# One block of a streaming encoder on one core: kept tiles' products tied to the gate matmuls on TensorE's queue, another first pair of groups for the dense stage, and GpSimd's share of the gate operands

## The chip, the cores and the metric

The kernel runs on one core of a Trainium2 chip. The metric is device microseconds for one execution; the kernel before was timed in three runs. PE is TensorE, DVE VectorE, ACT ScalarE, POOL GpSimd, SP the engine whose queue issues most plain DMAs.

## The reference, cut to what matters

The block computes a token mixer (an mLSTM beside a forgetting attention) and then a product-key expert layer (PEER) over 1024 tokens. The change touches only the PEER layer:

```python
# x: (1024, 1024); u_emb, v_emb: (16384, 1024)
scores = einsum('thpc,hpnc->thpn', (xb @ w_query), keys)     # 8 heads, 2 halves, 128 keys
val, idx = top_k(scores, 16)
top_s, pos = top_k(val[:, :, 0, :, None] + val[:, :, 1, None, :], 16)
ids  = idx0 * 128 + idx1 at pos                              # 8*16 = 128 experts per token
gate = softmax(top_s)
act  = gelu(einsum('ted,td->te', u_emb[ids], xb))
out  = einsum('te,ted->td', gate * act, v_emb[ids])
```

An expert's number is i * 128 + j. All is float32.

## The kernel before

The 1024 tokens are four segments of 256 (`SEGS`, two blocks of 128 tokens each). Segments 0 and 3 take the expert layer sparsely: each block gathers its 128 rows of u and 128 rows of v per token with indirect DMAs that POOL issues (`gather_rows`, L328, L364, L395), and DVE or PE uses them (L337, L386, L410). Segments 1 and 2 (512 tokens together, `DENSE`) take it densely: for each of 128 *tiles* of 128 experts, PE makes the 128 x 512 products of u with the tokens, ACT applies gelu, DVE multiplies by a dense table of gates, and PE multiplies the result with the tile's rows of v.

A tile's products cost 24 matmuls (`feat_proj`, L292): every fp32 operand is split into a high part on ACT (`wh`, L281) and a low part (`wl`, on DVE at L286, or for every third on POOL at L284), and three products are made for each of eight slices. Of the 128 tiles 60 are *kept* (`SPILL`): their products are made early (`spill`, L1025), copied out of PSUM by ACT (L1027) and stored to DRAM (`wsd`). 36 of the 60 are made while segment 3 is mixed, 24 in the stage after it. The other 68 (`rest`) are made in the dense stage itself by `dense_u` (L1204).

The stage around the change is the `merge` at L1214, from about 1600 us to 2038 us. It interleaves three generators in program order: the top-k of segment 3 (8 steps), 24 kept tiles, and `all_gates` (16 steps). `merge` takes next the generator with the smallest (steps done + 0.5) / cost; the costs of kept tiles and gates are 24 and 16.

`gates` builds the dense table for segments 1 and 2. For four tokens at a time (a *quad*; 128 quads, eight to a step) it makes four one-hot operands B in one DVE instruction (L1171) and four operands A: the last by two ACT instructions (L1176, L1177), the others by DVE or POOL (L1180); how many POOL makes is `GPOOL`, one of four for segment 1 and none for segment 2. Four matmuls (L1182, eight records in the trace) form the quad in one PSUM bank, and ACT copies it into `G` (L1184). A and B have two buffers. After eight quads `G` goes to DRAM (`gd`, L1186, 2 MB).

The dense stage takes the tiles in 32 groups of four. The list `order` begins with two kept groups (`FIRST`) and then takes rest and kept in proportion. `dense_u` is called five tiles ahead (`AHEAD`), `acc` (the residual of the 512 tokens) is loaded (L1246), and then, group by group, `weights` loads that group's gates (`Gt`, L1252), multiplies and splits them (L1256 to L1260), further `dense_u` follow, and `dense_v` splits the rows of v and runs 96 matmuls (L1278), which DVE adds to `acc` (L1283). `beat` hands out 1.08 of the 512 gathers of segment 3 per beat, and each waits for the PE instruction last recorded in `seen["pe"]`.

The order on each engine's queue is not the program order: a planner lists instructions by priority (program order, unless `high_priority`) over a modelled timeline, and the queues then run in that fixed order, each waiting on semaphores. `tc.issue_after(x)` makes the planner put the instructions of the block that run on x's engine behind x; it adds no wait of its own. The gate matmuls stand under `high_priority`.

Of the kernel before, what the change touches and what calls it, by code (L numbers as in the profile page):

```python
# [19 lines left out]
P = 128  # L20
# [29 lines left out]
SHARE = 3  # L50
GRP = 4
AHEAD = 5
FIRST = 2
XB = 4
XU = 1
TOP0 = (0, 1, 0, 1)
SW = 1
GP0 = 5

GPOOL = (1, 0)  # L60
T3W = 1.2
GW = 1
T00 = 0
# [30 lines left out]
def _block_kernel(ctx, tc, nc, I, out, dbg):  # L94
# [44 lines left out]
    dve, act, pe, pool_e, sync = nc.vector, nc.scalar, nc.tensor, nc.gpsimd, nc.sync  # L139
# [102 lines left out]
    h2d = dp.tile([SEQ, D], F32, tag="h2d", name="h2d")  # L242
    xnd = dp.tile([SEQ, D], F32, tag="xnd", name="xnd")

    Xh = big.tile([P, KT, 2 * NX], F32R, tag="xh", name="xh")
    Xl = big.tile([P, KT, 2 * NX], F32R, tag="xl", name="xl")
# [6 lines left out]
    def rawt(name):  # L253
        return wp.tile([P, L], F32, tag="raw", name=name, bufs=RAW)
# [20 lines left out]
    def halves(src, share=0, tiles=1):  # L275

        raw = rawt("raw")[:, 0:1024]
        sync.dma_start(raw.rearrange("p (i c) -> p i c", i=tiles) if tiles > 1 else raw, src)
        h = wpart("wh")
        l = wpart("wl")  # L280
        seen["act"] = act.copy(h, raw)  # L281
        turn[0] += 2
        if share and turn[0] % (2 * share) == 0:
            pool_e.tensor_sub(l, raw, h.bitcast(F32))  # L284
        else:
            seen["dve"] = dve.tensor_sub(l, raw, h.bitcast(F32))  # L286
        return [(h[:, i * 512:(i + 1) * 512], l[:, i * 512:(i + 1) * 512]) for i in range(2)]
# [6 lines left out]
    def feat_proj(wsrc, xh, xl, c, o=None, share=0):  # L294

        if xl is not None:
            u = halves(wsrc, share)
        else:
            raw = rawt("raw")[:, 0:KT * P]
            sync.dma_start(raw, wsrc)  # L300
        if o is None:
            o = acc_bank("fp")[:, 0:c.stop - c.start]
        if xl is None:
            for k in range(KT):
                pe.matmul(o, raw[:, k * P:(k + 1) * P], xh[:, k, c], start=(k == 0), stop=(k == KT - 1))  # L305
            return o
        for k in range(KT):
            h, l = u[k // 4]
            kc = slice(k % 4 * P, (k % 4 + 1) * P)
            mm3(o, c, h[:, kc], l[:, kc], xh[:, k, :], xl[:, k, :], k == 0, k == KT - 1)  # L310
        return o
# [707 lines left out]
    DX = 2 * NX  # L1019
    wsd = dp.tile([P, P, DX], F32, tag="wsd", name="wsd")  # L1020

    def spill(lo, hi):

        for i in range(lo, hi):
            a = feat_proj(I["ut"][i], Xh, Xl, slice(0, DX), share=SHARE)  # L1025
            t = ring("spill")[:, 0:DX]
            act.copy(t, a)  # L1027
            sync.dma_start(wsd[i], t)
            yield
# [101 lines left out]
    nb, xb0, nx = 2 * NB, sum(SEGS[:DENSE[0]]), DX  # L1131
# [4 lines left out]
    def gates(S, gb):  # L1136

        for b in range(NB):
            hi = gb.tile([P, P], I32, tag="gi", name="gi_hi")
            lo = gb.tile([P, P], I32, tag="gi", name="gi_lo")  # L1140
            dve.tensor_scalar(hi, S.idx[:, b, :], 7, None, op0=OP.logical_shift_right)
            dve.tensor_scalar(lo, S.idx[:, b, :], 127, None, op0=OP.bitwise_and)
            T = []
            for x, nm in ((hi, "iT"), (lo, "jT"), (None, "gT")):
                if x is None:
                    f = S.gate[:, b, :]
                else:
                    f = gb.tile([P, P], F32, tag="gf", name="gf", bufs=1)
                    dve.tensor_copy(f, x)
                tb = bank("gtr")  # L1150
                with tc.high_priority():
                    pe.transpose(tb[:, 0:P], f, ident)
                t_ = gb.tile([P, P], F32, tag=nm, name=nm, bufs=1)
                act.copy(t_, tb[:, 0:P])
                T.append(t_)
            iT, jT, gT = T
            niT = gb.tile([P, P], F32, tag="niT", name="niT", bufs=1)
            act.mul(niT, iT, -1.0)
            ngT = gb.tile([P, P], F32, tag="ngT", name="ngT", bufs=1)
            act.mul(ngT, gT, -1.0)  # L1160
            for tg in range(P // TG):
                G = gb.tile([P, P, TG], F32, tag="G", name="G")
                for q in range(TG // 4):
                    bk = dps.tile([P, 512], F32, tag="db", name="gout")
                    t0 = tg * TG + q * 4
                    ts4 = slice(t0, t0 + 4)
                    A = gb.tile([P, 4, P], F32, tag="A", name="A")
                    B = gb.tile([P, 4, P], F32, tag="B", name="B")
                    bc = [P, 4, P]
                    io = iota.unsqueeze(1).broadcast_to(bc)  # L1170
                    dve.tensor_tensor(B, io, jT[:, t0:t0 + 4].unsqueeze(2).broadcast_to(bc), op=OP.is_equal)  # L1171
                    for u in range(4):
                        t1 = slice(t0 + u, t0 + u + 1)
                        if u == 3:

                            act.activation(A[:, u, :], iota, AF.Abs, bias=niT[:, t1])  # L1176
                            act.activation(A[:, u, :], A[:, u, :], AF.Relu, bias=gT[:, t1], scale=ngT[:, t1])  # L1177
                        else:
                            e = pool_e if u < GPOOL[S.sg - DENSE[0]] else dve
                            e.tensor_scalar(A[:, u, :], iota, iT[:, t1], gT[:, t1], op0=OP.is_equal, op1=OP.mult)  # L1180
                        with tc.high_priority():
                            pe.matmul(bk[:, u * P:(u + 1) * P], B[:, u, :], A[:, u, :], start=True, stop=True)  # L1182
                    with nullcontext():
                      act.copy(G[:, :, q * 4:q * 4 + 4].rearrange("p i t -> p t i"),  # L1184
                             bk.rearrange("p (t i) -> p t i", t=4))
                sync.dma_start(gd[:, :, (NB * (S.sg - DENSE[0]) + b) * (P // TG) + tg, :].rearrange("g j c -> j g c"),  # L1186
                               G.rearrange("p (g i) t -> p g (i t)", i=GRP))
                yield


    kept, rest = list(range(sum(SPILL) // GRP)), list(range(sum(SPILL) // GRP, P // GRP))
    order = kept[:FIRST]
    kept = kept[FIRST:]
    while kept or rest:
        order.append((kept if len(kept) * (P // GRP) >= len(rest) * (P // GRP) and kept else rest).pop(0))

    def dense_u(i):
        i = order[i // GRP] * GRP + i % GRP
        w = up.tile([P, 512], F32, tag="w", name="w")
        if i < sum(SPILL):  # L1200
            sync.dma_start(w, wsd[i])
            act.activation(w, w, AF.Gelu)
        else:
            a = feat_proj(I["ut"][i], Xh, Xl, slice(0, nx), acc_bank("du"))  # L1204
            act.activation(w, a, AF.Gelu)  # L1205
        return w
# [24 lines left out]
    def beat(n=1):  # L1231

        count[0] += n * RATE
        k, count[0] = int(count[0]), count[0] % 1
        pace.step(seen["pe"], k)

    ws = []
    for i in range(AHEAD):
        ws.append(dense_u(i))
        beat(2)  # L1240

    ds_ = pool("dense", 2, reuse_waits="tile")
    xs0 = xb0 * P
    acc = ds_.tile([P, nb, D], F32, tag="acc", name="acc", bufs=1)
    for b in range(nb):
        sync.dma_start(acc[:, b, :], h2d[xs0 + b * P:xs0 + (b + 1) * P, :])  # L1246

    def weights(g):

        res = []  # L1250
        Gt = ds_.tile([P, nx // TG, GRP, TG], F32, tag="Gt", name="Gt", bufs=2)
        sync.dma_start(Gt, gd[order[g]].rearrange("j b (i t) -> j b i t", i=GRP))  # L1252
        for ii in range(GRP):
            w = ws[g * GRP + ii]
            w3 = w.rearrange("p (b t) -> p b t", t=TG)
            dve.tensor_mul(w3, w3, Gt[:, :, ii, :])  # L1256
            Wh = ds_.tile([P, 512], F32R, tag="Wh", name="Wh", bufs=2 * GRP)
            Wl = ds_.tile([P, 512], F32R, tag="Wl", name="Wl", bufs=2 * GRP)
            act.copy(Wh, w)  # L1259
            dve.tensor_sub(Wl, w, Wh.bitcast(F32))  # L1260
            res.append((Wh, Wl))
        return res

    def dense_v(g, W):
        for d in range(2):
            cv = slice(d * 512, (d + 1) * 512)
            bks = [bank("vo") if b < 2 else dps.tile([P, 512], F32, tag="db", name="vo") for b in range(nb)]
            for ii in range(GRP):
                if ii % 2 == 0:

                    e0 = (order[g] * GRP + ii) * P
                    v2 = halves(I["peer_v"][e0:e0 + 2 * P, cv].rearrange("(i p) c -> p i c", p=P), tiles=2)
                Wh, Wl = W[ii]
                vh, vl = v2[ii % 2]
# [10 lines left out]
    NG = P // GRP  # L1285
    for g in range(NG):
        W = weights(g)
        for i in range(len(ws), min(P, (g + 1) * GRP + AHEAD)):
            ws.append(dense_u(i))
            beat(2)  # L1290
        dense_v(g, W)
    pace.end()
# [50 lines left out]
```

## Time and profile before

| | |
|---|---|
| timed runs | 3248.06, 3258.47, 3261.81 us; median 3258.47 |
| profiled execution | 3247.17 us, span 3245.2 us |
| PE busy | 2943.9 us, 91% |
| DVE busy | 2345.9 us, 72% |
| POOL busy | 1407.1 us, 43% |
| ACT busy | 1047.9 us, 32% |
| DMA | 937.42 MB, 289 GB/s over the span |

The shares are means over stages that differ. PE's row by slices (each 81 us long) shows where it isn't full; the windows and waits of such a stretch then show what it waits for. A matmul's duration in a row overlaps with its neighbours', so the pace of PE is read from the distance of starts.

### The profile page before, as it was taken

The page shows a single profiled execution, that of the slowest core. Times are in us where ns is not written, and L with a number is a line of the kernel's source. Part 1 is how long each engine was busy: PE and PEld are TensorE (multiplying, and loading weights), DVE is VectorE, ACT ScalarE, POOL GpSimd, SP SyncE. Part 2 cuts the span into 40 slices and gives each one's busy share as a digit, 9 for nine tenths or more (in the row PEclk, how much of TensorE's full clock was granted, in tenths as well). Part 3 has the DMA queues.
Part 4 walks back from the last instruction along what each step waited for, and adds up shares of the span by engine and source line. Part 5 has one row for each costly group of instructions (what it writes and reads, how often), then busy time and mean ns, then how long its engine had stood idle before and what let it go on. Part 6 is the DMA issues. An engine that isn't in the chain of part 4 may idle for free. (4 is left out here: it accounts for less than half of the span.)

```text
span 3245.2 us, 40750 instructions
## 1 busy us (share of the span) xinstructions
PE 2943.9 (91%) x13711; PEld 2174.8 (67%) x13711; DVE 2345.9 (72%) x5633; ACT 1047.9 (32%) x1946; POOL 1407.1 (43%) x1221
## 2 busy tenths in 40 slices
PE   8999898667977889999899996898999999999998
PEld 4566566544654667776467885677777776777776
DVE  3342599997546897556467997788988877787787
ACT  1323323222222222222156666222332222232221
POOL 1000053554556654346465202345555555545454
PEclk9988998788979789999999997999999999999999
DMA  4534578998999978889997568889999998999888
GB/s 130 148 101 125 181 264 263 341 339 299 347 303 376 316 272 254 254 262 346 344 327 234 178 190 277 309 297 347 364 354 358 354 349 335 350 361 351 324 338 291
DMA packets 379317, 937.42 MB, mean 289 GB/s; under 512 B 57652, under 2 KB 143892, under 8 KB 375012
## 3 DMA queue, kind: packets, MB, share of 16 engines
q0 software_dynamic: 161216, 552.56, 47.9%
q1 hardware_dynamic: 217892, 382.25, 34.5%
q8 instruction: 108, 1.77, 0.2%
q14 instruction: 101, 0.83, 0.1%
HBM read 864.06 MB, written 70.62 MB: 288 GB/s over the span
## 5 line engine op out<-in xcount | busy, mean ns | idle before, releaser
L328 POOL DMA_INDIRECT gu<-in_peer_u,idx x512 | 626.1, 1223 | 622.0 <-PE vo L1278 123.5
L337 DVE SCALAR_TENSOR_TENSOR gu<-gu,xng 128x1024 f32<-128x1024 f32 x512 | 621.0, 1229 | 82.3 <-DMA gu<-in_peer_u,idx 81.2
L364 POOL DMA_INDIRECT gv<-in_peer_v,idT x384 | 426.0, 1109 | 410.4 <-PE po L386 193.4
L281 ACT CAST wh<-raw 128x1024 fp32r<-128x1024 f32 x288 | 301.3, 1048 | 674.2 <-PE vo L1278 329.4
L286 DVE TENSOR_TENSOR wl<-raw,wh 128x1024 fp32r<-128x1024 f32 x258 | 314.6, 1220 | 130.9 <-ACT wh L281 129.8
L1278 PE MATMUL vo<-wl,Wh 128*128 128x512 f32 x1024 | 403.7, 394 | 2.8 <-DVE wl L286 2.6
L1278 PE MATMUL vo<-wh,Wl 128*128 128x512 f32 x1024 | 400.4, 392 | 0.0
L1278 PE MATMUL vo<-wh,Wh 128*128 128x512 f32 x1024 | 360.0, 395 | 36.1 <-ACT Wh L1259 20.1
L305 PE MATMUL fp<-hnh,raw 128*128 128x256 f32 (+1 forms) x1024 | 250.6, 401 | 38.5 <-DVE frs L661 21.7
L1278 PEld LDWEIGHTS vo<-wh,Wh 128*128 128x128 f32 x1024 | 193.4, 190 | 92.3 <-ACT Wh L1259 20.3
L305 PEld LDWEIGHTS fp<-hnh,raw 128*128 128x128 f32 x1024 | 200.7, 200 | 80.7 <-DVE frs L661 23.3
L386 PE MATMUL po<-gv,Z 128*32 128x512 f32 x1536 | 213.9, 625 | 18.7 <-DMA gv<-in_peer_v,idT 18.1
L1278 PEld LDWEIGHTS vo<-wl,Wh 128*128 128x128 f32 x1024 | 193.7, 189 | 55.3 <-DVE wl L286 7.9
L1278 PEld LDWEIGHTS vo<-wh,Wl 128*128 128x128 f32 x1024 | 193.7, 189 | 44.3 <-issue 4.2
L292 PE MATMUL du<-xh,wl 128*128 128x512 f32 x544 | 214.2, 394 | 9.5 <-DVE wl L286 9.4
L292 PE MATMUL du<-xh,wh 128*128 128x512 f32 x544 | 214.6, 394 | 4.2 <-ACT wh L281 3.3
L395 POOL DMA_INDIRECT gr<-in_peer_v,idx x128 | 152.2, 1189 | 152.4 <-DVE gsum L410 50.8
L292 PE MATMUL du<-xl,wh 128*128 128x512 f32 x544 | 213.7, 393 | 0.0
L1283 DVE TENSOR_TENSOR acc<-acc,vo 128x512 f32<-128x512 f32 x256 | 167.1, 681 | 50.1 <-PE vo L1278 49.9
L292 PE MATMUL fp<-xh,wh 128*128 128x512 f32 x480 | 194.1, 404 | 4.6 <-ACT wh L281 4.4
L292 PE MATMUL fp<-xh,wl 128*128 128x512 f32 x480 | 192.2, 401 | 2.7 <-POOL wl L284 2.7
L461 PE MATMUL tk<-raw,hnh 128*128 128x512 f32 (+1 forms) x416 | 192.4, 609 | 1.5 <-DMA raw<-in_wt 1.0
(408 smaller groups left out, 5365.7 us busy)
## 6 DMA issues: line engine op xcount, KB each, us to landing
raw<-in_ut SPq DMA_DIRECT2D x128, 512.0 KB, 7.1
raw<-in_peer_v SPq DMA_DIRECT2D x128, 512.0 KB, 8.9
raw<-in_wf SPq DMA_DIRECT2D x64, 512.0 KB, 4.3
gd<-G SPq DMA_DIRECT2D x16, 2048.0 KB, 9.7
Gt<-gd SPq DMA_DIRECT2D x32, 1024.0 KB, 10.5
raw<-in_wt SPq DMA_DIRECT2D x48, 512.0 KB, 6.8
raw<-in_wq SPq DMA_DIRECT2D x48, 512.0 KB, 6.5
raw<-in_wo SPq DMA_DIRECT2D x32, 512.0 KB, 6.4
```

The costliest lines, as they stand in the source:

```text
L281: seen["act"] = act.copy(h, raw)
L286: seen["dve"] = dve.tensor_sub(l, raw, h.bitcast(F32))
L292: seen["pe"] = pe.matmul(o, w, x[:, c], start=(first and i == 0), stop=(last and i == 2))
L305: pe.matmul(o, raw[:, k * P:(k + 1) * P], xh[:, k, c], start=(k == 0), stop=(k == KT - 1))
L328: d = pool_e.indirect_dma_start(out=t, out_offset=None, in_=I["peer_u"], in_offset=bass.IndirectOffsetOnAxis(ap=S.idx[:, lb, r:r + 1], axi ...
L337: dve.scalar_tensor_tensor(t, t, 1.0, xn[0], op0=OP.mult, op1=OP.mult, accum_out=G.actv[:, r:r + 1])
L364: d = pool_e.indirect_dma_start(out=t, out_offset=None, in_=I["peer_v"], in_offset=bass.IndirectOffsetOnAxis(ap=S.idT[lb][:, tok:tok + 1], ...
L386: last = pe.matmul(G.po[32 * q_:32 * q_ + 32, n, :], z[:, q_, 31 - j:63 - j], rows[q_][:, n * 512:(n + 1) * 512], start=(j == 0), stop=(j ...
L395: d = pool_e.indirect_dma_start(out=t, out_offset=None, in_=I["peer_v"], in_offset=bass.IndirectOffsetOnAxis(ap=S.idx[:, lb, r:r + 1], axi ...
L461: pe.matmul(b[0:w, :], xh[:, k, s0:s0 + w], raw[:, k % 2 * 512:(k % 2 + 1) * 512], start=(k == 0), stop=(k == KT - 1))
L1278: seen["pe"] = pe.matmul(bks[b], w[:, cw], v, start=(ii == 0 and i == 0), stop=(ii == GRP - 1 and i == 2))
L1283: dve.tensor_add(o, o, bks[b])
```

## The change

Kept tiles' matmuls that are called once gates have been traced are queued on PE behind the gate matmul four quads back (`behind(4)`). The first five `dense_u` are queued behind the last gate matmul (`behind(0)`). `order` begins with a rest group and then a kept group, in place of two kept groups. POOL makes one A of four for both dense segments. The loads of `acc` are called after the first group's `weights`.

```diff
-FIRST = 2
-GPOOL = (1, 0)
+GPOOL = (1, 1)
...
+    gouts = []
+
+    def behind(n):
+
+        return tc.issue_after(gouts[-1 - 4 * n].ins) if len(gouts) > 4 * n else nullcontext()
+
     def spill(lo, hi):
 
         for i in range(lo, hi):
-            a = feat_proj(I["ut"][i], Xh, Xl, slice(0, DX), share=SHARE)
+            with behind(4):
+                a = feat_proj(I["ut"][i], Xh, Xl, slice(0, DX), share=SHARE)
...
-                            pe.matmul(bk[:, u * P:(u + 1) * P], B[:, u, :], A[:, u, :], start=True, stop=True)
+                            gouts.append(pe.matmul(bk[:, u * P:(u + 1) * P], B[:, u, :], A[:, u, :],
+                                                   start=True, stop=True))
...
-    order = kept[:FIRST]
-    kept = kept[FIRST:]
+    order = [rest.pop(0), kept.pop(0)]
...
     for i in range(AHEAD):
-        ws.append(dense_u(i))
+        with behind(0):
+            ws.append(dense_u(i))
         beat(2)
...
-    for b in range(nb):
-        sync.dma_start(acc[:, b, :], h2d[xs0 + b * P:xs0 + (b + 1) * P, :])
...
     for g in range(NG):
         W = weights(g)
+        if g == 0:
+            for b in range(nb):
+                sync.dma_start(acc[:, b, :], h2d[xs0 + b * P:xs0 + (b + 1) * P, :])
```

## Rows read from the trace of the kernel before

**Rows 1.** The page, PE's busy tenths in 40 slices of the span.
```profile
PE   8999898667977889999899996898999999999998
```
**Rows 2.** Windows of the gate stage: length, busy per engine, PE clock, DMA, GB/s.
```profile
1600.00:1835.00 235.00, 215.95 (x1278) 167.72 (x1271) 171.16 (x559) 136.06 (x248) 132.41 (x118) 0.96 0.80 267
1835.00:1955.00 120.00, 118.64 (x686) 104.16 (x685) 109.70 (x368) 81.58 (x148) 12.65 (x8) 1.00 0.64 194
1955.00:2018.00 63.00, 42.50 (x228) 37.35 (x227) 56.05 (x138) 48.99 (x87) 17.44 (x15) 0.76 0.82 291
```
**Rows 3.** Windows of the gate matmuls alone (L1182): PE, weight loads.
```profile
1835.00:1955.00 120.00, 38.97 (x296) 37.84 (x296) 1.00 0.64 194
1955.00:2018.00 63.00, 41.89 (x224) 37.02 (x224) 0.76 0.82 291
```
**Rows 4.** Groups on ACT from 1835 to 1955 us: count, busy, mean ns, idle before.
```profile
L281 ACT CAST wh<-raw 128x1024 fp32r<-128x1024 f32 x11 | 11.5, 1046 | 8.2 <-PE fp L292 7.7 <-issue 0.5
L1027 ACT COPY spill<-fp 128x512 f32<-128x512 f32 x11 | 6.4, 579 | 0.1
```
**Rows 5.** Waits from 1955.6 to 2038 us, the longest.
```profile
DVE w L1256 <- DMA Gt<-gd: 20.4, 1, 20.4
```
**Rows 6.** PE's timeline: start, length, line, count, idle before.
```profile
1942.83 1.95 PE L1182 MATMUL gout<-A,B 128*128 128x128 f32 x16
1944.53 0.48 PE L292 MATMUL fp<-xh,wl 128*128 128x512 f32 x1
...
2038.13 0.79 PE L1278 MATMUL vo<-wh,Wh 128*128 128x512 f32 x1 [20.07 <-ACT Wh L1259]
...
2041.71 1.90 PE L1278 MATMUL vo<-wh,Wl 128*128 128x512 f32 x4
2043.41 0.42 PE L1278 MATMUL vo<-wh,Wh 128*128 128x512 f32 x1
```
**Rows 7.** ACT's timeline, two gate copies one quad apart.
```profile
2004.28 1.02 ACT L1184 COPY G<-gout 128x512 f32<-128x512 f32 x1
...
2005.94 1.03 ACT L1184 COPY G<-gout 128x512 f32<-128x512 f32 x1
```
**Rows 8.** DVE's timeline, one quad's operands without a pause.
```profile
1998.47 0.85 DVE L1180 TENSOR_SCALAR A<-iota,iT,gT 128x128 f32<-128x128 f32 x3
1999.23 0.68 DVE L1171 TENSOR_TENSOR B<-iota,jT 128x512 f32<-128x512 f32 x1
1999.84 0.85 DVE L1180 TENSOR_SCALAR A<-iota,iT,gT 128x128 f32<-128x128 f32 x3
```
**Rows 9.** Groups on DVE, first from 1608 to 1835, then from 1955 to 2018 us.
```profile
L1171 DVE TENSOR_TENSOR B<-iota,jT 128x512 f32<-128x512 f32 x65 | 48.2, 743 | 38.7 <-PE gout L1182 38.2 <-ACT jT L1154 0.4
L1180 DVE TENSOR_SCALAR A<-iota,iT,gT 128x128 f32<-128x128 f32 x128 | 40.4, 359 | 0.0
...
L1180 DVE TENSOR_SCALAR A<-iota,iT,gT 128x128 f32<-128x128 f32 x78 | 22.4, 341 | 0.0
L337 DVE SCALAR_TENSOR_TENSOR gu<-gu,xng 128x1024 f32<-128x1024 f32 x16 | 19.1, 1214 | 4.1 <-DMA gu<-in_peer_u,idx 4.1
L1171 DVE TENSOR_TENSOR B<-iota,jT 128x512 f32<-128x512 f32 x26 | 17.8, 684 | 1.3 <-PE gout L1182 1.2
```
**Rows 10.** Groups on POOL, first from 1608 to 1835, then from 1835 to 1955 us.
```profile
L1180 POOL TENSOR_SCALAR A<-iota,iT,gT 128x128 f32<-128x128 f32 x64 | 71.2, 1115 | 78.4 <-PE gout L1182 51.3 <-issue 5.8 <-DVE cand L945 4.3
...
L284 POOL TENSOR_TENSOR wl<-raw,wh 128x1024 fp32r<-128x1024 f32 x3 | 7.6, 2522 | 83.0 <-ACT wh L281 83.0
```
**Rows 11.** The DMA queue's timeline between the two stages.
```profile
2019.73 7.80 SPq L1246 DMA_DIRECT2D acc<-h2d  x4
2029.16 10.41 SPq L1252 DMA_DIRECT2D Gt<-gd  x3
```
**Rows 12.** The chain that ended last, one piece in mid dense stage.
```profile
2746.81 21.76 PE vo L1278 x96
```
**Rows 13.** Waits of PE alone, 2018 to 2310 us.
```profile
PE vo L1278 <- DVE acc L1283: 14.0, 5, 3.6
```

## The prediction

> **What bounds the kernel now.** I read the page's slices first, for where PE isn't full. Its row is 9 nearly throughout, and the deepest hole is the pair 6 and 5 in the 25th and 26th slices, 1947 to 2110 us [rows 1]; the dense stage behind it is full. So what the change is worth there is time in which PE stands still. The windows of that stretch come next. From 1835 to 1955 PE is busy 118.6 of 120 us, and DVE 109.7; from 1955 to 2018 PE is down to 42.5 of 63 us at a granted clock of 0.76, while DVE is at 56.0 and ACT at 49.0 [rows 2]. The window of the gate matmuls alone says what is left then: 296 records before 1955 and 224 after, at eight to a quad 37 quads and 28 of 128, so 63 were done by 1835 [rows 3]. ACT copied 11 kept tiles between 1835 and 1955 [rows 4], hence 13 of the 24 by 1835 and all by 1955. PE has used up its filling work, and the last 28 quads run at the pace of ACT and DVE. Then comes a second hole: the last gate matmul ends at 2018.06, and PE starts the first `vo` 20.07 us later [rows 6], because DVE waits 20.4 us for `Gt` [rows 5], which goes to DRAM and back.
>
> What PE really lost: 28 quads cost it 23.8 us at full pace (16 records in 1944.53 - 1942.83 = 1.70 us, 0.85 a quad [rows 6]), and from 1955.6 to 2038.1 it spent 82.5. So 58.7 us are there to be won, and 19 of the 235 us before 1835 [rows 2].
>
> **Part 1, the turns.** From `merge`'s costs, kept tile k (counted from 0) is called after the smallest number j of eight-quad steps with (k + 0.5)/24 <= (j + 0.5)/16, and is put behind quad 8j - 4. Tile 11 comes behind 60 quads, tile 12 also 60, tile 19 behind 100, tile 20 behind 108, tile 23 behind 124. Before, 13 tiles stood beside 63 quads at 1835: that already fits the turns, so I take the stage up to 1835 as unchanged. From there on the turns bind: 24 tiles were done by 100 quads, and only 20 may be.
>
> **Part 2, POOL's A.** One quad's A now costs DVE two instructions, not three. Three take 1999.23 - 1998.47 = 0.76 us, and B 0.61 [rows 8], so one A is worth 0.25. Beside POOL's A the two are longer: B 743 against 684 ns, A 359 against 341 [rows 9], 59 + 2 x 18 = 95 ns a quad. Saved: 0.155 us a quad; a quad's DVE time becomes 1.20. For POOL it's 65 quads x 1.115 us [rows 10] = 72 us, where it was busy 12.7 of 120 [rows 2], so POOL has the room. The bounds are +0.25 us a quad (no interference) and a loss of 1.02 (the last rival). I take the measured 0.155, which comes from the same pair of instructions.
>
> The Trainium skill (SBUF — State Buffer, Who interferes with whom) says that GpSimd and a VectorE instruction with two SBUF inputs or in a two-port mode lock each other out for the whole instruction. This trace shows B and A longer by 59 and 18 ns beside a POOL A of 1115 ns, so far less than a whole instruction on average; by the rule taken at its worst the quad would cost DVE time instead of saving it, the last rival below.
>
> **Part 3, when the gates end.** From 1835 to 1955 DVE, busy 109.7 of 120 us, gives out 37 quads; the 37 x 0.155 = 5.7 us saved give 5.7/1.20, nearly 5 more: 42, in all 105. The turns then allow 20 kept tiles, 7 in this stretch for 11 before. A tile's 24 matmuls cost PE 24 x 21.76/96 = 5.44 us [rows 12], so PE has 4 x 5.44 less to do here (and no early dense tile) and will be seen waiting, some 20 us. After 1955 are left 23 quads and 4 tiles. ACT: 2005.94 - 2004.28 = 1.66 us a quad [rows 7], and 1.05 + 0.58 a tile [rows 4]: 38.2 + 6.5 = 44.7 us. PE: 23 x 0.85 + 4 x 5.44 = 41.3. DVE: 23 x 1.20 and three low parts, about 31; the 16 gathered rows that took 19.1 us of it [rows 9] now wait for later PE instructions. ACT ends last: the gates end at 1999.7, not 2018.1. Bounds: if PE stays as full as before 1955, it needs 118.6 - 5.5 + 23.8 = 137 us from 1835 on, so 1972; if the turns only hand the hole on to the middle, 2018.
>
> What queues behind a kept tile that waits: on PE top-k's products and later gates; on ACT the tile's copy, and since `wh` has two buffers the next tile's cast, with gate copies behind it. I price that by the ACT sum being taken without a gap shared with PE.
>
> **Part 4, the first rest group.** Four made tiles are queued behind the last gate: 4 x 5.44 = 21.8 us of PE work. The round trip was 20.07 us after the last gate matmul [rows 6], so it lies beneath with 1.7 to spare. `vo` starts at 1999.7 + 21.8 = 2021.5, 16.6 us earlier than 2038.1. And four made tiles are behind it by then, where one was before: 3 x 5.44 = 16.3 us that leave the dense stage. The first 12 `vo` ran at half clock, four in 43.41 - 41.71 = 1.70 us [rows 6], 0.425 each for 0.227, after 20 us of idleness; with PE busy right before, that's 2.4 us more. If the cover fails (a `Gt` slowed by the made tiles' u and the gathers), it costs what the trip takes beyond 21.8.
>
> **Part 5, the rest.** `acc` took the SP queue for 7.8 us while `Gt` had to wait for `gd` anyway, until 2029.16 [rows 11]; behind `Gt` it now holds up v's loads instead, 0 to 7.8 us; I take 0, as the ring of four raw buffers lets two of them load before the gates end. The changed order: before, two kept groups and then four rest groups ran first, and PE waited 14.0 us for DVE's `acc` adds up to 2310 [rows 13]; alternation may remove those 14, the 19.1 us of DVE work that moves in may add as much. I take 4 us gained.
>
> **Sum.** 16.6 + 16.3 + 2.4 + 4 = 39.3 us. The profiled execution took 3247.2 (span 3245.2 and 2.0 around it), so 3207.9 by its own time; the median of the timed runs is 11.3 above it. 3258.5 - 39.3 = 3219.2, say 3219.
>
> **Rivals.**
> - *PE never starves.* The planner fills the turns with top-k's products and the other engines keep up, so the gates end at 1972, 28 us earlier than forecast: 3191. For it: PE and DVE were both over 90% busy from 1835 to 1955 [rows 2], so the two can run together. Against: the turns take four tiles from that very stretch.
> - *The gates end no sooner.* A and B have two buffers, and each engine in turn waits for the next; the end stays at 2018 and only part 4 pays: 39.3 - 18.4 = 20.9, 3238. For it: ACT was at 49 of 63 us in the tail [rows 2] and gains nothing from POOL.
> - *Slower: POOL's A behind a waiting low part.* POOL makes every third tile's low part, and waited 83.0 us for `wh` before three of these between 1835 and 1955 [rows 10], with nothing behind. Now each A queued behind such a wait stops its quad; the quad stops the tile queued behind it, whose matmuls must free `wh`. The waits then stand in a circle that only the planner's order breaks. It decides from 39 us of stalls on; all 83 give 3219 + 83 = 3302. Against it: the planner puts the low part where its model has `wh` ready, and before 1835 POOL waited 51.3 us for gate matmuls [rows 10] without holding PE up for as long (19 us idle in all [rows 2]).
> - *The lock.* Each POOL A blocks DVE for its whole 1.115 us: 1.02 us a quad beyond the forecast's 0.095, 65 quads, 66 us of DVE. From 1955 on DVE has 44.7 - 31 = 13.7 to spare, so 53 us: 3272. Against it: the 59 and 18 ns.
>
> **How the numbers follow.** Forecast 0.50, PE never starves 0.20, gates no sooner 0.17, POOL's queue 0.08, the lock 0.05. The forecast's own range is 3203 to 3236: gates 10 us sooner or SP, DVE and `Gt` costing 17. For 8 in 10 I reach from 3185 (PE full, with part of the 14.0 us) to 3250 (gates no sooner, with 12 of the unknown costs), which leaves out the two slow rivals and a little of the fast one. About 0.5%, 16 us, is what a measurement of this kernel can tell from no change, so faster means below 3242: the forecast less 0.02, the first rival, and 0.10 of the second, 0.78. Same: 0.02 + 0.07 + 0.03 of the lock, which lies at its edge, 0.12. Slower: 0.10.
>
> **What would show it.** Right: kept tiles' matmuls still beside gates in the last 40 us before the last gate matmul; that one near 2000 us; `du` matmuls in the 20 us behind it and no wait of PE for `Wh` there; DVE's A 256 in place of 320. Wrong in the step: the last gate later than 2018 with POOL's A as what PE waits for (third rival), or B near 1.5 us on the mean (the lock). The whole is wrong if PE's idle time from 1835 to the first `vo` isn't lower by some 40 us, or if it comes back in the dense stage as waits for DVE or `Gt`.

## The result, and the profile after

The changed kernel took 3239.74 us (median; 3231.14 to 3255.49) where the kernel before took 3258.45: a ratio of 0.9945 [0.9934, 0.9956], 18.7 us faster. The forecast was 39.3. In a later group of runs the same pair gave 0.9965 [0.9947, 0.9984]. The kernel before alone had medians from 3245.1 to 3260.1 us on the five chips of the experiments, so below a kernel is compared only with those of its own group of runs.

The profiled execution of the changed kernel has a span of 3230.7 us (before 3245.2). The hole is gone from PE's slices: the 25th and 26th are 8 and 8 where 6 and 8 stood [rows 1]. (The prediction read the second of them as 5; the pair of 6 in the 8th and 9th slices is deeper, and the sum doesn't go by either.)

```profile
PE   8899888767988889999899998899999999999997
```

The windows of the gate stage answer [rows 2] (length, busy of PE, PEld, DVE, ACT and POOL, PE's clock, DMA share, GB/s):

```profile
1600.00:1835.00 235.00, 215.57 (x1307) 163.74 (x1306) 170.02 (x544) 145.09 (x271) 137.08 (x123) 0.98 0.81 273
1835.00:1955.00 120.00, 112.48 (x658) 98.79 (x657) 104.55 (x361) 83.27 (x152) 53.03 (x45) 0.99 0.58 176
1955.00:2018.00 63.00, 57.05 (x314) 48.02 (x314) 34.91 (x73) 42.02 (x71) 29.50 (x24) 1.00 0.65 201
2018.00:2060.00 42.00, 34.52 (x141) 28.03 (x141) 27.84 (x43) 12.84 (x19) 16.63 (x14) 0.88 1.03 412
```

From 1955 to 2018 PE is busy 57.05 us for 42.50, at full clock for 0.76. DVE fell from 56.05 to 34.91 there, and the DMA share from 0.82 to 0.65: the gathers of segment 3 left this stretch, and in the next one the transfers are full (1.03). PE's timeline shows the last gate matmul at 1998.8, made tiles (`du`) right behind it, and the first `vo` at 2026.20 with no wait, where 20.07 us of idleness stood [rows 6]. The next wait is 7.48 us for the first `acc` add:

```profile
1998.63 0.49 PE L1188 MATMUL gout<-A,B 128*128 128x128 f32 x2 [0.38 <-ACT A L1183]
1998.88 0.47 PE L291 MATMUL du<-xh,wh 128*128 128x512 f32 x1
...
2025.98 0.39 PE L291 MATMUL du<-xh,wl 128*128 128x512 f32 x1
2026.20 1.07 PE L1283 MATMUL vo<-wh,Wh 128*128 128x512 f32 x4
...
2044.72 0.77 PE L1283 MATMUL vo<-wh,Wh 128*128 128x512 f32 x1 [7.48 <-DVE acc L1288]
```

So PE got its lead. How much of it lasts is read by counting `du` and `vo` matmuls from 1900 us on, each at the 0.227 us of full pace (us of dense work done by a time; a few per cent of records can be missing):

```
by            2040   2060   2100   2200   2300   2400   2600   3200
before         6.3   21.8   60.1  149.4  238.7  331.9  507.8 1036.0
changed       38.1   50.8   82.7  168.2  259.6  345.5  523.0 1056.6
lead          31.8   29.0   22.6   18.8   20.9   13.6   15.2   20.6
```

32 us of lead at 2040 are some 20 by 2200. The count leaves out the matmuls for gathered rows, so it isn't the whole of PE's work: by the last `vo` of the high parts (`wh`, `Wh`; "the last `vo`" from here on), which began at 3209.2 for 3235.3, 26.1 are left at the end. But PE isn't last any more, and the span is only 14.5 shorter. After it DVE still adds gathered rows, and waits for their transfers (DVE's timeline of the changed kernel, then of the kernel before, which had no such wait):

```profile
3216.98 2.60 DVE L409 SCALAR_TENSOR_TENSOR gsum<-gr,wr,gsum 128x1024 f32<-128x1024 f32 x2
3221.11 1.28 DVE L409 SCALAR_TENSOR_TENSOR gsum<-gr,wr,gsum 128x1024 f32<-128x1024 f32 x1 [1.54 <-DMA gr<-in_peer_v,idx]
3223.62 1.28 DVE L409 SCALAR_TENSOR_TENSOR gsum<-gr,wr,gsum 128x1024 f32<-128x1024 f32 x1 [1.22 <-DMA gr<-in_peer_v,idx]
3225.64 1.28 DVE L409 SCALAR_TENSOR_TENSOR gsum<-gr,wr,gsum 128x1024 f32<-128x1024 f32 x1 [0.74 <-DMA gr<-in_peer_v,idx]
```

```profile
3235.92 1.88 DVE L1283 TENSOR_TENSOR acc<-acc,vo 128x512 f32<-128x512 f32 x3
3237.72 2.60 DVE L410 SCALAR_TENSOR_TENSOR gsum<-gr,wr,gsum 128x1024 f32<-128x1024 f32 x2
```

From the last `vo` to the end of the span, the *tail*, it is 21.5 us now, and was 9.9. Two questions follow: which part of the change made the lead, and why the gathers of segment 3 (512 indirect loads, spread over the dense stage) now end last. The theory tried below ("gathers" in the expectations) is that they moved out from beneath the gates into a stretch where transfers and DVE are full.

### The profile page after: what moved, and what is told of

Its sections match the earlier page's. It is cut to its first block, busy times and chain, and to the rows that moved or that the text cites. A ratio compares the mean times of both kernels' runs of the same rounds, so it can differ in the third digit from the quotient of the medians.

```text
span 3230.7 us, 40854 instructions
## 1 busy us (share of the span) xinstructions
PE 2937.6 (91%) x13711; PEld 2164.8 (67%) x13711; DVE 2327.7 (72%) x5569; ACT 1045.1 (32%) x1946; POOL 1488.1 (46%) x1285
## 5 line engine op out<-in xcount | busy, mean ns | idle before, releaser
L327 POOL DMA_INDIRECT gu<-in_peer_u,idx x512 | 637.3, 1245 | 542.5 <-DVE gu L336 147.5
L363 POOL DMA_INDIRECT gv<-in_peer_v,idT x384 | 418.4, 1090 | 411.4 <-PE po L385 190.1
L385 PE MATMUL po<-gv,Z 128*32 128x512 f32 x1536 | 211.8, 626 | 17.0 <-DMA gv<-in_peer_v,idT 16.2
L1186 POOL TENSOR_SCALAR A<-iota,iT,gT 128x128 f32<-128x128 f32 x128 | 144.5, 1132 | 152.5 <-PE gout L1188 106.8
```

What stands on the lines that cost most here:

```text
L327: d = pool_e.indirect_dma_start(out=t, out_offset=None, in_=I["peer_u"], in_offset=bass.IndirectOffsetOnAxis(ap=S.idx[:, lb, r:r + 1], axi ...
L363: d = pool_e.indirect_dma_start(out=t, out_offset=None, in_=I["peer_v"], in_offset=bass.IndirectOffsetOnAxis(ap=S.idT[lb][:, tok:tok + 1], ...
L385: last = pe.matmul(G.po[32 * q_:32 * q_ + 32, n, :], z[:, q_, 31 - j:63 - j], rows[q_][:, n * 512:(n + 1) * 512], start=(j == 0), stop=(j ...
```

## Experiments

**One part undone at a time** (one chip, kernel before 3258.82). GpSimd's A as before:

```diff
-GPOOL = (1, 1)
+GPOOL = (1, 0)
```

> The changed kernel, but POOL makes one A of four for segment 1 alone, as before. Theory (the lead of 33 us that PE has at 2038 us is lost later, to the gathers of segment 3 that no longer run beneath the gates: DMA and DVE full from 2000 to 2310 us, and the gathers ending after PE): DVE gets 64 more A of 0.25 us less 0.095 of interference each, the gates end at 2000 to 2010, and the time is 3238 to 3248. Rival (POOL's A itself eats the gain, PE waited 34 us for it): the gates end no later and the time is 3225 to 3233.

The kept tiles' products not queued in turns:

```diff
-            with behind(4):
+            with nullcontext():
```

> The changed kernel without the turns: kept tiles' products may again run ahead of the gates. Theory (gathers): the gates end some 15 us later, at 2010 to 2018, but the later stages give only part of an earlier end on, so the time is 3243 to 3250. If instead all of the gates' earlier end reaches the end (so that the loss has another cause), 3255 to 3260. If the turns cost as much in the middle as they give, 3235 to 3242.

Two kept groups first, as before:

```diff
-    order = [rest.pop(0), kept.pop(0)]
+    order = kept[:2]
+    kept = kept[2:]
```

> The changed kernel with the old order: two kept groups first, so nothing is made behind the last gate. Theory (gathers): the gates end near 2000, PE then stands 20 us for Gt, but the first 18 gathers again start beneath the gates and the second group's loads don't collide; 3236 to 3248. Rival (the order itself is what loses the lead, since the kept group's stored products are loaded late): the loss of 14 us from 2038 to 2100 is gone and the time is 3222 to 3232.

The `acc` loads issued ahead of the first `Gt`, as before:

```diff
+    for b in range(nb):
+        sync.dma_start(acc[:, b, :], h2d[xs0 + b * P:xs0 + (b + 1) * P, :])
...
-        if g == 0:
-            for b in range(nb):
-                sync.dma_start(acc[:, b, :], h2d[xs0 + b * P:xs0 + (b + 1) * P, :])
```

> The changed kernel with the loads of acc where they were, ahead of the first Gt. Theory (gathers): 2 MB of some 19 MB that DMA moves from 1999 to 2050 us come earlier, hardly anything changes, 3236 to 3243. Rival (acc's loads behind Gt hold up v's first rows, for which PE waits 7.5 us at 2037): 3228 to 3234, and no wait of PE there.

Measured: without GpSimd's A 3243.54 us (0.9952 [0.9935, 0.9968]), without the turns 3238.61 (0.9938 [0.9917, 0.9959]), with the old order 3264.94 (1.0023 [1.0004, 1.0042]), with the early `acc` loads 3235.90 (0.9926 [0.9908, 0.9944]). Only the order carries the gain: undone, it costs all of it and more. That missed both of its ranges (3236 to 3248 and 3222 to 3232): the turns stay in that kernel, and without the order they do harm, as the next runs show. The run without the turns missed the theory's 3243 to 3250, and that with the early `acc` loads lies at the lower edge of 3236 to 3243. The intervals of the other three overlap, and no changed kernel ran beside them. GpSimd did take work from DVE, as these groups of the gate stage show (the changed kernel, then the one without its A: count, busy, mean ns, idle before), 173.3 us for 190.1, 16.8 in the 64 quads concerned; but DVE stood idle some 50 us before B in either, and the stage took 382.7 us with and without, so DVE's time wasn't what the quads waited for:

```profile
L1177 DVE TENSOR_TENSOR B<-iota,jT 128x512 f32<-128x512 f32 x128 | 90.3, 707 | 59.3 <-PE gout L1188 57.2 <-ACT jT L1160 1.2 <-PE fp L291 0.4
L1186 DVE TENSOR_SCALAR A<-iota,iT,gT 128x128 f32<-128x128 f32 x256 | 83.0, 363 | 0.8 <-ACT gT L1160 0.8
```

```profile
L1186 DVE TENSOR_SCALAR A<-iota,iT,gT 128x128 f32<-128x128 f32 x320 | 96.9, 351 | 0.0
L1177 DVE TENSOR_TENSOR B<-iota,jT 128x512 f32<-128x512 f32 x128 | 93.2, 729 | 50.3 <-PE gout L1188 48.2 <-ACT jT L1160 1.2 <-PE fp L291 0.5
```

**One part alone.** The turns alone in the kernel before (only `behind(4)` around the kept tiles' products; kernel before 3245.08 on this chip), and, on another chip (3251.84), the order alone:

> The kernel before with the turns alone. The forecast's step: the gates end 12 to 18 us earlier (DVE still makes three A in segment 2), 2000 to 2006, then 20 us of waiting for Gt as before. If an earlier end of the gates reaches the end in full: 3241 to 3246. Theory (gathers, whose first 18 still start beneath the gates here): half or more of it, 3242 to 3251.

```diff
-    order = kept[:FIRST]
-    kept = kept[FIRST:]
+    order = [rest.pop(0), kept.pop(0)]
...
-        ws.append(dense_u(i))
+        with tc.issue_after(gouts[-1].ins):
+            ws.append(dense_u(i))
```

> The kernel before with the order of the dense tiles alone changed (a group still to be made first, its tiles' products behind the last gate). Theory (this part carries the gain; the turns give nothing, GpSimd's A 4 us): 14 to 20 us faster than the kernel before, a ratio of 0.994 to 0.9957. Rival (the parts need each other): under 8 us faster.

The turns alone are slower: 3256.70 us, 1.0037 [1.0020, 1.0054]. The order alone is 20.7 us faster: 3231.15, 0.9935 [0.9916, 0.9954], all of the gain and a little over the 14 to 20 expected, so the parts don't need each other. The turns alone missed both of their ranges (3241 to 3251). The turns alone do bring the last gate forward, from 2017.7 to 1992.6; PE then waits 45.8 us for its first `Wh`. The DMA queue's timeline says why. The first five tiles' gathers wait for the last kept product, which the turns put at the gates' end; released there all at once, they fill the transfers (share 1.05 from 1994 to 2023), and SP takes 28.19 us to issue the five loads of kept tiles, 25.48 of them for the first. The `gd` store issued at 1994.23, on which `Gt` depends, is slow as well: behind those loads SP still waits for a `gd`, until 2026.4. So the loads alone don't explain the late `Gt`. The first fence is that timeline, the second the waits from 1992 to 2042 (the last line is of SP's own):

```profile
1994.23 0.37 SPq L1192 DMA_DIRECT2D gd<-G  x1
1994.65 28.19 SPq L1207 DMA_DIRECT2D w<-wsd  x5
...
2028.74 13.33 SPq L1258 DMA_DIRECT2D Gt<-gd  x3
```

```profile
PE vo L1284 <- ACT Wh L1265: 45.8, 1, 45.8
ACT w L1208 <- DMA w<-wsd: 29.0, 2, 27.1
DVE w L1262 <- DMA Gt<-gd: 19.1, 1, 19.1
SPq L1252 <- DMA gd<-G: 2.6, 1, 2.6
```

What shortened the gate stage? First B and last weight load of a gate matmul (ns min/median/max, first and last start) of the kernel before, of the order alone and of the turns alone:

```profile
L1171 DVE TENSOR_TENSOR B<-iota,jT x128: 661/684/2923, 1608.0 to 2014.8; 128x512 f32<-128x512 f32 x128
L1182 PEld LDWEIGHTS gout<-A,B x1024: 186/192/338, 1620.6 to 2017.7; 128*128 128x128 f32 x171
```

```profile
L1173 DVE TENSOR_TENSOR B<-iota,jT x128: 669/687/2918, 1611.8 to 1992.4; 128x512 f32<-128x512 f32 x128
L1184 PEld LDWEIGHTS gout<-A,B x1024: 186/192/333, 1620.9 to 1995.3; 128*128 128x128 f32 x171
```

```profile
L1177 DVE TENSOR_TENSOR B<-iota,jT x128: 628/683/2657, 1606.1 to 1987.2; 128x512 f32<-128x512 f32 x128
L1188 PEld LDWEIGHTS gout<-A,B x1024: 186/192/338, 1615.7 to 1992.6; 128*128 128x128 f32 x171
```

From the first B to the last gate it is 409.7 us before, 383.5 with the order alone and 386.5 with the turns alone (382.7 in the changed kernel). Neither turns nor GpSimd's A are needed for it. Common to the short ones is that DVE's work on the first 16 gathered rows, 19.1 us [rows 9], comes behind the gates and not beneath them. That is about half of it: the kernel before without any gathers (the next experiment, one execution) still took 396.8 us, by the rows below. What made up the other half isn't shown; a made tile that ran before the last gates (24 `du` matmuls from 1948 us) also moved to their end or behind it.

```profile
L1171 DVE TENSOR_TENSOR B<-iota,jT x128: 668/684/1636, 1608.1 to 2002.1; 128x512 f32<-128x512 f32 x128
L1182 PEld LDWEIGHTS gout<-A,B x1024: 185/192/334, 1620.5 to 2004.9; 128*128 128x128 f32 x171
```

**Without the gathers.** Both kernels with no gathers of segment 3 at all (its output gets the residual alone), on the chip of the turns alone:

```diff
-    pace = Paced(gather_items(segs[-1], GS3, room3), LAG)
+    pace = Paced(iter(()), LAG)
...
```

> The kernel before without segment 3's expert layer: its 512 gathers and what uses them are left out of the dense stage, its output rows get the residual alone. Beside the next kernel it tells where the lead goes. Both theories: some 100 us faster than before, 3140 to 3180, since PE's 512 small matmuls (59 us) and its waits go.

> The changed kernel without segment 3's expert layer, as the kernel above. Theory (gathers): the lead of 33 us that PE has when its first v products start isn't lost any more, so it is 28 to 38 us faster than the kernel before without that layer. Rival (order, loads of acc or of stored products, POOL): the difference stays at 14 to 20 us.

3097.57 us for the kernel before, far below the 3140 to 3180 expected, and 3071.24 for the changed one: 26.3 apart, a little under the 28 to 38. The lead in dense work was 26.8 us at 2040 and 26.7 at 2800, and the last `vo` began 26.7 earlier. Without gathers PE loses nothing, as a window of the changed one shows:

```profile
2100.00:2300.00 200.00, 200.00 (x884) 165.58 (x884) 108.75 (x135) 66.22 (x87) 0.00 (x0) 1.00 0.42 144
```

With them PE is busy 187.14 of these 200 us. Then both kernels without 18 of the 512 gathers, late ones, beside the changed kernel itself (kernel before 3260.12):

```diff
+            left = [] if S is not segs[-1] else B.v[108:112] + B.v[113:127]
...
-                yield from rest[2 * i:2 * i + 8]
+                yield from (x for x in rest[2 * i:2 * i + 8] if x not in left)
```

> The changed kernel as it is, for the comparison with the other three kernels on one chip. Both theories: a ratio of 0.994 to the kernel before (0.990 to 0.998).

> The changed kernel without 18 of the 512 gathers of segment 3 (18 of the v rows of its second block, all of them among the last 55 in the order of issue; their share of the output is left out), so nothing of it differs before about 3100 us. Theory (in the changed kernel the gather stream ends last: its last sum came 16 us after TensorE's last dense matmul, the end 21.5 us after it): 18 gathers at some 2.3 us each (21.7 of them in 50 us) take the stream's lateness away, the tail after TensorE falls from 21.5 to about 9 us, and the time falls by 10 to 20 us. Rival (TensorE alone sets the end, and a tail of 20 us follows it anyway): the tail stays and the time falls by 0 to 4 us.

> The kernel before without the same 18 gathers (their share of the output is left out). Theory: there the stream ended with TensorE (9.3 us from the last dense matmul to the end), so it gains 0 to 6 us only, and the two kernels with 18 gathers fewer lie 26 to 32 us apart instead of 18.7. Rival (the gathers cost both kernels the same, as a load on VectorE and the transfers): both gain alike, within 4 us, and the distance stays at 15 to 22 us.

The changed kernel: 3250.08 us. Without 18 gathers 3233.93, 16.2 us less, and the tail is 7.2 us for 21.6, as the theory said. The kernel before gave 3253.61, 6.5 less, a little over the 0 to 6. The two are 19.7 us apart for 10.0 with all gathers: the gathers do cost the changed kernel more, but the expected distance of 26 to 32 was missed. That the stream sets the end is shown; that its last 18 are the whole of the loss is not.

**Where the first gathers start.** In the first of these kernels the first five tiles' gathers wait for the last kept product instead of PE's latest matmul (chip of 3245.08):

```diff
-    def beat(n=1):
+    def beat(n=1, by=None):
...
-        pace.step(seen["pe"], k)
+        pace.step(by or seen["pe"], k)
+
+    first = seen["pe"]
     ws = []
     for i in range(AHEAD):
         with behind(0):
             ws.append(dense_u(i))
-        beat(2)
+        beat(2, first)
```

> The changed kernel, but the gathers that the first five dense tiles hand out wait for the last kept tile's product (the PE instruction before the dense stage) and not for the made tiles. Theory (gathers): ten of them run beneath the gates' end as before, the stretch from 2000 to 2060 us is less full, PE keeps 5 to 10 us more of its lead of 33, the last gather ends 5 to 15 us earlier: 3226 to 3236. Rival (something other than the gathers costs the lead): 3237 to 3243.

It gave 3238.03 us (0.9983 [0.9969, 0.9998]), outside the 3226 to 3236 expected, and no changed kernel ran beside it. It tells little of the theory: with the turns the last kept product itself came at 1988, so nearly all of the gathers stayed behind the gates. So the turns had to go first. `v12_both` is the changed kernel with two of the edits above, no turns and early `acc` loads; it ran beside the three kernels with the 18 gathers:

> The changed kernel without the turns (products of the kept tiles issued at once again) and with the acc loads at their old place; the early tiles still to be made and GpSimd's A stay. Each of the two alone was 1 and 4 us faster than the changed kernel. Theory (the turns give nothing once dense tiles cover the wait for Gt, and the acc loads are in nobody's way there): 2 to 8 us faster than the changed kernel on the same chip. Rival (what the two showed was chance): within 2 us of it.

3237.43 us (0.9929 [0.9912, 0.9946]), 12.7 below the changed kernel on that chip, more than the 2 to 8 expected: turns and late `acc` loads together do cost something. On the chip of the order alone it was the base for two single edits, the early gathers of the diff above, and LAG = 3 for 5 (a gathered row is used 3 beats after its request):

> The changed kernel without the turns and with the acc loads at their old place once more, beside the other three on one chip. Both theories: a ratio to the kernel before of 0.993 (0.990 to 0.996).

> The kernel without the turns (acc loads at their old place) in which the gathers of the first five tiles wait for the last kept tile's product, so they start near 1956 us, beneath the gates' tail as in the kernel before, and not near 2005. Theory (the gather stream ends last because its first 18 gathers were moved from a stretch with idle transfers into one where they are full): its tail after TensorE falls from 20 to about 10 us, the gates end up to 13 us later, and the time falls by 0 to 10 us against the same kernel without this. Rival (those gathers cost the gates' tail on VectorE what they save at the end): 0 to 8 us slower.

> The kernel without the turns (acc loads at their old place) with each gathered row used 3 beats after its request instead of 5, so that its buffer comes free some 4 us sooner. Theory A (the transfers, 93% busy, set the stream's pace): the same time within 4 us. Theory B (the eleven buffers, for which GpSimd waited some 280 of 700 us, set it): the stream ends 10 us or more sooner and the time falls by 5 us or more.

The base took 3229.90 us, with early gathers 3222.76 (0.9910 [0.9891, 0.9928]), with the shorter lag 3231.20 (0.9932 [0.9912, 0.9951]). The intervals overlap, so the 7.1 us of the early gathers are not clear of noise here. The base is level with the order alone (3231.15), so GpSimd's A adds nothing there either. The shorter lag gains nothing; the transfers are nearly full. These are the shares of 16 engines by queue in the changed kernel from 2300 to 2900 us (packets, MB, share):

```profile
q0 software_dynamic: 36566, 133.16, 58.7%
q1 hardware_dynamic: 29690, 77.21, 34.1%
```

A gather moves 0.524 MB (128 rows of 4 KB), so 18 of them are 9.4 MB, and at 133.16 MB in 58.7% of 600 us 25 us of all engines. Beneath the gates' tail the engines have that to give (0.65 busy); from 2018 to 2060 they have nothing (1.03). With the early gathers the gates ended 17.5 us later (2011.9 for 1994.4). This delay isn't DVE's. The timeline of GpSimd shows its A behind ten gathers in its queue, and PE's waits from 1950 to 2012 say the same (total, times, longest):

```profile
1948.09 1.03 POOL L327 DMA_INDIRECT gu<-in_peer_u,idx  x1 [2.30 <-PE idt L358]
...
1960.21 0.94 POOL L327 DMA_INDIRECT gu<-in_peer_u,idx  x1 [0.30 <-issue]
1961.18 1.58 POOL L1186 TENSOR_SCALAR A<-iota,iT,gT 128x128 f32<-128x128 f32 x2
...
1991.59 2.44 POOL L1186 TENSOR_SCALAR A<-iota,iT,gT 128x128 f32<-128x128 f32 x2 [0.93 <-PE gout L1188]
```

```profile
PE gout L1188 <- POOL A L1186: 26.0, 27, 12.3
```

**The best version**: that kernel once more, and with GPOOL = (1, 0), so that GpSimd has no A in this tail (chip of 3247.20):

> The kernel with the first gathers beneath the gates' tail once more (no turns, acc loads at their old place, GpSimd's A of four throughout), as the base on this chip. A ratio to the kernel before of 0.991 (0.989 to 0.994).

> The same kernel with GpSimd's A of four in the first dense segment only. In the profile of the former TensorE waited 12.3 us for a GpSimd A that stood behind ten gathers in GpSimd's queue (1948 to 1961 us), and then some 0.5 us in each of 27 quads. Theory (in this tail GpSimd's A is what the gates wait for): the gates end 10 to 16 us sooner, and with VectorE idle for 26 us there nothing takes its place; the time falls by 3 to 10 us. Rival (the full transfers after 2005 set the end, as where the gates ended 17 us sooner and the time was 7 us longer): within 3 us of the same.

3225.60 us (0.9938 [0.9916, 0.9960]) and 3214.29 (0.9893 [0.9873, 0.9913]): 11.3 us from one digit, a little over the 3 to 10 expected, and 32.9 below the kernel before. The first ratio is no better than the base's 0.9926 on the chip before, so nothing here shows the early gathers to pay beside GpSimd's A. This last kernel is the order alone with the early gathers and nothing else: 0.9893 [0.9873, 0.9913] for 0.9935 [0.9916, 0.9954], on two chips (32.9 us of gain for 20.7). The gates end at 1999.7 for 2011.1 (387.3 us from the first B, though ten gathers run beneath: their rows are used behind the gates), and what PE waits for in the tail is now ACT (waits from 1950 to 2110):

```profile
PE gout L1188 <- ACT G L1191: 10.6, 19, 3.1
PE vo L1286 <- DVE acc L1291: 5.1, 2, 4.7
```

Its windows show DVE at 39.39 of 45 us behind the gates, working on rows that had come during them; in the changed kernel it was 23.58 there:

```profile
1955.00:2005.00 50.00, 37.66 (x231) 32.29 (x231) 36.23 (x101) 42.73 (x78) 5.82 (x6) 0.93 0.75 249
2005.00:2050.00 45.00, 39.37 (x166) 31.83 (x165) 39.39 (x61) 16.95 (x23) 17.26 (x13) 0.96 1.03 382
```

The last `vo` began at 3206.5, and the span ended 8.6 us behind it, so the lead no longer goes into the tail.

## Why the prediction was half right

- **What bounds the kernel** held: the hole between 1955 and 2038 was what was to be had. That the dense stage behind it is simply "full" was the flaw: it is full on PE and nearly full on the DMA engines, and the second fullness stands in the DMA row of the slices of the kernel before, 8 or 9 from the 25th on, which the prediction didn't read:

```profile
DMA  4534578998999978889997568889999998999888
```

- **Part 1, the turns.** The kept tiles did stand beside the gates to the end (last copy at 1997.6), and 20 of them were copied by 1955, as forecast; but that gains nothing: a ratio of 0.9938 for 0.9945 when undone, and 11.6 us lost alone. They also move what is paced by the last kept product, the gathers. That consequence was not followed.
- **Part 2, GpSimd's A.** DVE saved 16.8 us in 64 quads, 0.26 each, the upper bound rather than 0.155. It reached no end: the gate stage took as long without. Beside gathers in GpSimd's queue it costs 11.3 us. The third rival had the right mechanism, an A behind something waiting on GpSimd, with the wrong thing ahead of it. The lock isn't seen between GpSimd's A and DVE's operands, and the 59 and 18 ns weren't its price either: they are differences of means, the median of B is 684 ns, and a few long B raise the mean. All four above 1 us in the kernel before ran beside GpSimd's low part (`wl`, another instruction with two inputs) and ended 0.55 us behind it. There B did wait until the other's end, as here (DVE, then GpSimd):

```profile
1837.19 2.85 DVE L1171 TENSOR_TENSOR B<-iota,jT 128x512 f32<-128x512 f32 x1
1836.69 2.81 POOL L284 TENSOR_TENSOR wl<-raw,wh 128x1024 fp32r<-128x1024 f32 x1 [4.64 <-ACT wh L281]
```

  The Trainium skill (SBUF — State Buffer, Who interferes with whom) has GpSimd and such a VectorE instruction lock each other out for a whole instruction. The trace agrees beside `wl` (2.85 us) and not beside A.
- **Part 3, the gates' end.** Forecast 1999.7, seen 1998.8, and the nearness is luck: the stage began 8 us later than before (1616.0 for 1608.0) and was 27.0 us shorter, not 18.4. Nor did it need what the prediction gave the credit to, turns and A: the order alone makes it 26.2 us shorter. About half of that is the 19.1 us of gathered rows leaving DVE, which the prediction took out of DVE's sum but gave no credit, as it let ACT set the end. In the kernel before PE waited for DVE's A (the first line, of its longest waits from 1955 to 2018); with the order alone (the second) it waits only for ACT, the limit that was forecast:

```profile
PE gout L1182 <- DVE A L1180: 13.5, 10, 5.0
PE gout L1184 <- ACT G L1186: 10.9, 25, 0.5
```

- **Part 4** held. Five made tiles (120 matmuls), not four, were made behind the last gate and lay over the trip of `Gt`, and `vo` began 27.4 us behind the gates with no wait. Four would not have done: DVE began on `Gt` only at 2021.84, 23.0 us behind the last gate, and four tiles cover 21.8. Parts 3 and 4 together promised 35.3 us at the first `vo`, and the lead at 2040 was 31.8.
- **Part 5 is the step that failed**: "alternation may remove those 14, the 19.1 us of DVE work that moves in may add as much. I take 4 us gained." The sum books nothing for the transfers, and takes it that what PE gains the end gains. In place of +4, the 35.3 us had become 26.1 by the last `vo`, and the tail, 21.5 us for 9.9, took 11.6 of these: 14.5 in the two profiles, 18.7 by the medians. The prediction's own sign of being wrong was there: PE's idle time from 1835 us to the first `vo` fell by 28.4 us (41.9 to 13.5) and not by some 40, and part of it came back as waits for DVE. From 2018 to 2310 PE's waits for `acc` adds fell from 14.0 [rows 13] to 7.5 us, but those for `wl` and `wh` rose from 3.2 to 18.9, two of them here:

```profile
PE du L291 <- DVE wl L285: 5.5, 5, 2.5
PE vo L1283 <- DVE wl L285: 5.3, 5, 2.5
```

  From 2100 to 2200 DVE is busy 93.42 us for 82.85, the DMA share 0.94 for 0.83, and PE 92.36 for 93.90 (before, then changed):

```profile
2100.00:2200.00 100.00, 93.90 (x395) 76.70 (x395) 82.85 (x124) 25.51 (x32) 44.39 (x35) 0.95 0.83 302
2100.00:2200.00 100.00, 92.36 (x379) 73.63 (x378) 93.42 (x144) 25.89 (x34) 62.34 (x45) 0.95 0.94 340
```

  Without gathers the lead stays whole (26.7 us). With the first ones back beneath the gates and GpSimd free for them, in a kernel without the turns, the gain is 33 us, near the 39.3. How the loss divides between dense stage and tail is that of one execution: with the turns undone, at a median as short, the tail was 9.6 us.
- **Two slips in the sums** that move nothing: a quad's 1.20 us is 1.22 by its terms (0.76 + 0.61 - 0.155), and gates 10 us sooner give 3209, not the range's 3203.
- **`acc` behind `Gt`** was booked at 0 to 7.8 us of loss, taken as 0. Its old place gave 0.9926 for 0.9945; the intervals overlap. PE's 7.48 us wait for the first `acc` add stood behind v's rows: ACT waited 11.05 us for them, until 2040.53, DVE 7.93 us for ACT's `wh`, and the add stands behind this on DVE. With the old place this wait is gone, and PE waits 6.7 us for a `Wh` instead.

What stays open: how the loss from 2040 to 2200 divides between DVE, with its gathered rows, and the late loads (ACT began on the stored tiles 24 to 30 us after the first of their loads was issued at 2021.84); and the other half of what shortened the gate stage. And profiled executions differ by up to 24 us before the gate stage begins (first B from 1601.5 to 1625.3), which no edit here explains.

## What to carry to other kernels

When a step moves, look for what is paced by it: here loads tied to "the latest matmul" or "the last kept product" moved with it, out of a stretch with idle transfers into one without. Put back, they turned 20.7 us of gain into 32.9, each on its own chip. Read the DMA row of the slices beside PE's before calling a stage bound by one engine, and ask which stream will end last if that engine gets faster. Look at the queue of a helping engine first: ten gathers ahead of GpSimd's A made PE wait 12.3 us here. And look at a median before taking a difference of two means for a price.

## What was not expected of the hardware

- With the DMA share at 1.05, SP took 28.19 us to issue five loads of 256 KB, 25.48 for the first, and all behind them on SP waited.
- DVE's B, 0.68 us by the median, took up to 2.92 us beside GpSimd's `wl`, and 0.69 by the median beside its A.
- Moving a DVE instruction of 0.35 us to GpSimd (1132 ns) 64 times left the gate stage as long as it was (382.7 us with and without).
- One kernel's medians on five chips lay 15 us apart (3245.1 to 3260.1), nearly as much as the effect measured.
